# Rounding weights in the background of a matmul stage: loads asked further ahead, four raw tiles and two high tiles in rotation

## The chip, the cores and the metric

One core of a Trainium2 chip. The metric is the device time of one execution in microseconds, as the median of three runs. The core has five engines with an instruction queue each: TensorE (PE: matmuls, and weight loads shown as PEld), VectorE (DVE), ScalarE (ACT), GpSimd (POOL) and SyncE (SP, which here only issues DMAs). Each engine works through its own queue in order and waits on semaphores for the others.

## The reference

One layer of a causal decoder: a half-step gated feed-forward network, two attention mixers in parallel, and a second half-step feed-forward network, on a sequence of 1024 rows of width 1024, all in float32.

```python
x = x + 0.5 * swiglu(rms_norm(x, g_ffn1), w1_gate, w1_up, w1_down)      # 1024 -> 2816 -> 1024
proj = rms_norm(x, g_mix) @ w_in                                        # one combined projection
# ... q, k, v and gates are columns of proj; attention a (sparse), attention b (stick-breaking) ...
x = x + (sigmoid(gate_a) * (y_a @ w_o_a) + sigmoid(gate_b) * (y_b @ w_o_b)) @ w_out
x = x + 0.5 * swiglu(rms_norm(x, g_ffn2), w2_gate, w2_up, w2_down)

def swiglu(h, w_gate, w_up, w_down):
    return (silu(h @ w_gate) * (h @ w_up)) @ w_down
```

## The kernel before, in words

Products are made in a reduced float32 format of the matmul engine. To keep the accuracy, every operand is split into a high part (a rounded copy) and a low part (what the rounding left), and one product of tiles is three matmuls: high by high, high by low and low by high (lines L468 to L470).

The kernel runs in stages. The one that matters here is the first gate and up stage, `ffn_in("a", ...)`: silu(h @ w1_gate) * (h @ w1_up). The 2816 columns are taken 256 at a time, as eleven pairs p of two 128-column blocks. The first pair is done plainly (`opening`). For each of the ten others the gate (e = 0) and the up half (e = 1) are each one fast matrix product of 2 x 2 blocks that takes 7 block products instead of 8 (`products`). A block product is `times`: 4 blocks of depth times 3 matmuls, 12 matmuls of 128x128 by 128x512. So the stage has 10 x 2 x 7 = 140 block products behind the opening, in sequences of seven. In a sequence the products have the places 0 to 6 (the order 1, 6, 7, 5, 2, 4, 3 of the fast scheme) and go to the PSUM banks pa, pb, pc, pd, pa, pc, pd. Between the places 0 and 4 ScalarE copies bank pa out (L481); between 3 and 6 VectorE adds bank pd to a sum (L491) before the product at place 6 goes on accumulating in it. VectorE also makes the sums of the next sequence's left sides (L457 to L460), ScalarE rounds these and the weights themselves (L377), GpSimd subtracts to get the low parts (L378). SyncE loads weights (L440, tiles a0r and a1r, 512 KB each) and stores finished results to DRAM (L594, `staged`).

Beside this work the stage does a background job (`beside`, called after each block product): it prepares 24 column blocks of w_in that later stages need, in high and low parts, in DRAM. They come in two pieces each, 48 pieces of 128x512. A piece goes through four steps:

- load: SyncE loads 256 KB into a raw tile `swr` (L799);
- split: ScalarE copies it rounded into a high tile `swh` (L789), and VectorE subtracts it from the raw tile in place, so that this then holds the low part (L790);
- store: SyncE stores the high part (L793, targets named ..hd) and the low part (..ld), one after the other.

`behind` ties a step to a block product: the load, the split's rounding and the store each wait for that product's last matmul. Before the change three slots take turns. A tuple in `points` gives the places of split, store and load of a slot:

```python
spare = in_turn((c3, 3), (c1, 1), (pair, 2))
held, points = {}, ((0, 1, 3), (2, 3, 5), (4, 5, 0))
```

So every sequence of seven products does three pieces: splits after the places 0, 2 and 4, each store one product behind its split, and the load of the slot's next piece two products behind that store, 4 products ahead of its own split. A slot has a raw tile and a high tile of its own, six tiles in all, handed out by `spare`. A load can't start before the store of the low part has left the raw tile.

Semaphores and the order of the instructions on each engine are made by a planner, from the traced order, the data dependences, the added ones of `behind`, and its own estimate of times. Only the opening is held to its written order as a whole, and a few instructions by `keep_in_program_order`.

Of the kernel before, what the change touches and what calls it, by code (L numbers as in the profile page):

```python
# [23 lines left out]
P = 128  # L24
# [33 lines left out]
def f32(ap):  # L58
    return ap.bitcast(F32)
# [186 lines left out]
def trunk(ctx, tc, x, positions, g_ffn1, w1_gate, w1_up, w1_down, g_mix, w_in, g_cq, w_uq_a, w_q_idx,  # L246
          g_q_a, g_k_a, w_uv_a, w_o_a, w_o_b, w_out, g_ffn2, w2_gate, w2_up, w2_down, inv_freq, out):
    nc = tc.nc
# [28 lines left out]
    def column(g, n, name):  # L277
        t = cst.tile([P, n], F32, name=name)
        nc.sync.dma_start(t, g[0].rearrange("(k p) -> p k", p=P))
        return t  # L280
# [31 lines left out]
    def in_turn(*sources):  # L312

        order = [f for n in range(max(n for f, n in sources)) for f, m in sources if n < m]
        at = [0]

        def tile_(name):
            at[0] += 1
            return order[(at[0] - 1) % len(order)](name)

        return tile_
# [59 lines left out]
    class Right:  # L381
# [16 lines left out]
        def place(self, xs, half, junk=None):  # L398

            self.x, self.half, self.junk, self.rs = xs, half, junk, {}  # L400
            for q in range(2):
                self.y[half, q] = ([xt[:, q * 512:q * 512 + 512] for xt in xs] if half else
                                   [self.ct(f"{self.nm}y{q}{t}") for t in range(4)])
# [33 lines left out]
    def loader(raw, nm):  # L437
        def load(w, f, name):
            t = raw(name)
            nc.sync.dma_start(t.rearrange("p (k f) -> p k f", k=ND),  # L440
                              w[0, :, f * P:(f + 1) * P].rearrange("(k p) f -> p k f", p=P))
            return t

        return load

    def ffn_in(nm, R, wg, wu, raw, op, sums, ct, bank, staged, rows, first=None, beside=lambda n, ins: None):
# [26 lines left out]
        def mul(O, n, ps, start=True):  # L473
            a, b = FACTORS[n]
            beside("1675243".index(str(n)), times(O[a], B[b], ps, start))
# [253 lines left out]
    columns = {f"wg{g}": C_GA + g * P for g in (*range(ND, 2 * ND), *range(ND))}  # L729
    columns.update((f"wqk{base}{pr}", base + pr * P) for pr in range(4) for base in (C_QB, C_KB))  # L730
    split_of = {nm: [dram.tile([P, 1024], F32, name=f"{nm}{part}d") for part in "hl"] for nm in columns}
    rows_of = w_in[0].rearrange("(k p) f -> p k f", p=P)
# [18 lines left out]
    def ring(pool):  # L751

        op = in_turn((wt, 4), (lambda name: pool.tile([P, 1024], F32R, tag="r", name=name, bufs=NR), NR))
        raw = in_turn((rawt, 2), (lambda name: pool.tile([P, 1024], F32, tag="raw", name=name, bufs=2), 2))
        return op, raw

    def of(pool, tag, bufs, n=1024, dt=F32):
        return lambda name: pool.tile([P, n], dt, tag=tag, name=name, bufs=bufs)
# [3 lines left out]
    with tc.tile_pool(name="ring1", bufs=1) as rpool, tc.tile_pool(name="s1", bufs=1) as spool, tc.tile_pool(name="ps1", bufs=1, space=PSUM) as psum:  # L762
        op, raw = ring(rpool)
        bank = banks(psum)
        sums, pair = of(spool, "s", 5, 512), of(spool, "pair", 2, 512, F32R)
        with tc.tile_pool(name="t1", bufs=1, side="right") as tpool, tc.tile_pool(name="c1", bufs=1) as cpool:
            tt = of(tpool, "t", 28, dt=F32R)
            fp = lambda place: lambda name: f32(place(name))

            c4, c5, c3, c1 = (of(cpool, f"c{n}", n, 512, F32R) for n in (4, 5, 3, 1))  # L770
            ct = fp(in_turn(*[(f, 1) for f in [c4] * 4 + [c5] * 5]))
            spare = in_turn((c3, 3), (c1, 1), (pair, 2))
            R = Right(g_ffn1, bank, fp(op), fp(in_turn((c5, 5), (c3, 3))), tt, "a")
            xs = []

            pieces = [(nm, c) for nm in columns for c in range(0, 1024, 512)]
            held, points = {}, ((0, 1, 3), (2, 3, 5), (4, 5, 0))

            def behind(ins, *others):
                for o in others:  # L780
                    tc.add_manual_dep(o.ins, ins.ins.name, mybir.DependencyInfo(
                        mybir.DependencyClass.Sync, mybir.DependencyReason.DATA), reason="pace")

            def beside(n, ins):

                for slot, (split_, store, load_) in enumerate(points):
                    if n == split_ and slot in held:
                        nm, c, raw, hi = held[slot]
                        behind(ins, nc.scalar.activation(hi, raw, AF.Copy))  # L789
                        nc.vector.tensor_tensor(raw, raw, f32(hi), op=ALU.subtract)  # L790
                    if n == store and slot in held:
                        nm, c, raw, hi = held.pop(slot)
                        behind(ins, *(nc.sync.dma_start(d[:, c:c + 512], part)  # L793
                                      for d, part in zip(split_of[nm], (f32(hi), raw))))
                    if n == load_ and pieces:
                        nm, c = pieces.pop(0)
                        raw, hi = f32(spare(f"swr{slot}")), spare(f"swh{slot}")
                        held[slot] = nm, c, raw, hi
                        behind(ins, nc.sync.dma_start(raw.rearrange("p (k f) -> p k f", f=P),  # L799
                                                      rows_of[:, c // P:(c + 512) // P, columns[nm]:columns[nm] + P]))  # L800

            def rows(t):
                xs.append(fp(tt)(f"x{t}"))
                nc.sync.dma_start(xs[t], x[0, t * P:(t + 1) * P, :])

            load = loader(raw, "a")
            for t in range(4):
                rows(t)
                if t == 1:
                    R.gain()  # L810
            first = [[load(w, q, f"a{e}r0") for q in range(2)] for e, w in enumerate((w1_gate, w1_up))]
            for t in range(4, NT):
                rows(t)
            gcolm = column(g_mix, ND, "gcolm")
            gcolq = column(g_cq, QR // P, "gcolq")
            gk = cst.tile([P, HD], F32, name="gk")
            nc.sync.dma_start(gk, g_k_a[0].partition_broadcast(P))

            R.place(xs[0:4], 0)
            R.stat(0)  # L820
            for t in range(4):
                if t < 3:
                    R.stat(t + 1)
                R.norm(t)
            R.second = lambda: R.place(xs[4:8], 1, sums)
            ffn_in("a", R, w1_gate, w1_up, raw, op, sums, ct, bank, staged[0], range(4), first, beside)
            assert not held and not pieces
        hpool.append(tc.tile_pool(name="hpool", bufs=1, side="right"))
        hstack = ExitStack()
        hpool[0] = hstack.enter_context(hpool[0])  # L830
# [129 lines left out]
    fp = tc.tile_pool(name="sf", bufs=1)  # L960
# [1055 lines left out]
    with tc.tile_pool(name="ring2", bufs=1) as rpool, tc.tile_pool(name="ps6", bufs=1, space=PSUM) as psum:  # L2016
        op, raw = ring(rpool)
        bank = banks(psum)
        with tc.tile_pool(name="m0", bufs=1) as mpool:
            M0 = []  # L2020
            for d in range(0, ND, 2):
                wh, wl = first.pop(0) if first else wcols(w_o_a, d * P, 2 * P, 0, 4, f"woa{d}")
                for e in range(2):
# [5 lines left out]
                    for k in range(4):  # L2029
                        c = slice((2 * k + e) * P, (2 * k + e + 1) * P)  # L2030
# [9 lines left out]
            fp = lambda place: lambda name: f32(place(name))  # L2040
# [132 lines left out]
```

## Time and profile before

| | us |
|---|---|
| median of 3 runs | 2239.9 |
| range of the runs | 2239.87 to 2240.59 |
| profiled execution, its own time | 2240.86 |
| its span, first to last instruction | 2239.1 |
| mean granted TensorE clock | 0.989 of full |
| TensorE busy, of the span | 97% |
| VectorE, ScalarE, GpSimd busy | 68%, 49%, 38% |

Rows of the profile name a line (L789 is line 789 of the kernel), an engine, an operation, and output tile <- input tiles with their buffer numbers left out. An engine name with q (SPq) is its instruction queue. In a row of a group stand the count, the busy time in us with the mean duration of one in ns, and the time for which the engine sat idle just before these instructions, with what ended most of that time. In a row of the timeline stand start and duration in us, and in brackets the idle time before the instruction and what ended it. In a row of waits stand the total, the number of times and the longest, in us. The releasers are inferred: of several semaphores the row names the one that came last by the profile.

### The profile page before, as it was taken

The numbers are of one execution on the slowest core, as the hardware profiler recorded it, in microseconds if no ns is written. First come the engines' busy times: TensorE is split into PE (matmuls) and PEld (weight loads), VectorE is DVE, ScalarE is ACT, GpSimd is POOL, SyncE is SP. The second block draws the span as 40 slices with busy tenths as digits, with TensorE's granted clock in tenths as the row PEclk, the third lists the DMA queues.
The fourth block names the chain that finished last, engine by engine and source line by source line (L and its number), as shares of the span: only waits on it lengthen the run. The fifth ranks groups of instructions, "written<-read, shape, count | busy, mean of one in ns | idle before, by whom it ended". The sixth has DMA issues, their size and how long they took to land.

```text
span 2239.1 us, 30578 instructions
## 1 busy us (share of the span) xinstructions
PE 2169.2 (97%) x10460; PEld 1807.1 (81%) x10460; DVE 1526.3 (68%) x2548; ACT 1104.4 (49%) x2169; POOL 858.2 (38%) x698
## 2 busy tenths in 40 slices
PE   7999999999999999899999899999999999999999
PEld 6887787788878988788788788877888888888877
DVE  5675675687875498677788688853465564668685
ACT  4333333334445258999989466533333232233443
POOL 3355455532236344211111322255245454552233
PEclk9999999999999999999999999999999999999999
DMA  5376676688686333665554623566223233349755
GB/s 171 99 216 199 205 239 190 195 286 275 198 219 177 111 118 126 195 176 170 151 160 164 209 95 99 170 218 236 67 77 117 90 113 97 115 160 324 229 165 184
DMA packets 269052, 381.01 MB, mean 170 GB/s; under 512 B 23264, under 2 KB 157040, under 8 KB 268896
## 3 DMA queue, kind: packets, MB, share of 16 engines
q1 hardware_dynamic: 256384, 339.17, 48.9%
q0 software_dynamic: 12512, 39.89, 4.9%
q8 instruction: 82, 1.34, 0.2%
q14 instruction: 74, 0.61, 0.1%
HBM read 259.94 MB, written 119.05 MB: 169 GB/s over the span
## 4 chain that ended last, share of the span: by engine, by line
PE 70%; ACT 7%; DVE 6%; DMA 4%; issue 3%; POOL 2%; SPq 0%; ACTq 0%; POOLq 0%; DVEq 0%
PE p L681 6%; PE p L682 6%; PE p L680 6%; ACT junka L1186 3%; PE pd L468 3%; PE pd L469 3%; PE pd L470 3%; PE pc L470 3%; PE pc L468 3%; PE pc L469 3%; PE pa L469 3%; PE pa L468 3%; PE pa L470 3%; PE psf L308 2%; PE psf L309 2%
## 5 line engine op out<-in xcount | busy, mean ns | idle before, releaser
L1186 ACT ACTIVATE junka<-u,cand,sig 128x768 bf16<-128x768 f32 (+4 forms) x186 | 183.8, 988 | 5.6 <-DVE cand L1183 4.0
L790 DVE TENSOR_TENSOR swr<-swr,swh 128x512 f32<-128x512 f32 x48 | 45.8, 954 | 111.2 <-ACT swh L789 107.2
L789 ACT ACTIVATE swh<-swr 128x512 fp32r<-128x512 f32 x48 | 30.2, 630 | 165.6 <-DMA swr<-in_w_in_dram 56.5
L1627 DVE TENSOR_TENSOR_SCAN left<-left 128x640 f32<-128x640 f32 (+3 forms) x64 | 86.3, 1349 | 4.0 <-ACT left L1619 4.0
L1120 POOL DMA_DIRECT2D gd<-evg x32 | 17.9, 560 | 152.6 <-ACT evg L1117 112.7
L1676 DVE TENSOR_TENSOR pt<-pstT,pt 128x512 fp32r<-128x512 f32 (+1 forms) x96 | 50.8, 549 | 28.6 <-ACT pt L1674 28.3
L584 ACT ACTIVATE b0u<-b0u 128x512 f32<-128x512 f32 x20 | 12.7, 633 | 95.3 <-DVE b0u L491 78.9
L1676 DVE TENSOR_TENSOR pt<-pspT,pt 128x512 fp32r<-128x512 f32 x72 | 46.8, 684 | 16.3 <-ACT pt L1674 16.3
L681 PE MATMUL p<-bT,bS 128*128 128x512 f32 x132 | 52.5, 398 | 2.4 <-DVE bT L378 2.4
L1674 ACT ACTIVATE pt<-pspT 128x512 fp32r<-128x512 f32 x72 | 39.7, 596 | 29.2 <-PE pspT L1886 29.1
L1807 ACT ACTIVATE e<-e,nm 128x256 f32<-128x256 f32 (+7 forms) x64 | 49.3, 773 | 9.3 <-DVE nm L1802 9.2
L1540 DVE SCALAR_TENSOR_TENSOR u<-relu,WI,u 128x512 f32<-128x512 f32 (+1 forms) x70 | 50.1, 733 | 5.2 <-ACT relu L1533 4.6
L1795 DVE CUSTOM_DVE_ANT_0 e<-psL,bias 128x512 f32<-128x512 f32 (+3 forms) x96 | 49.7, 550 | 5.5 <-PE psL L1832 5.5
L682 PE MATMUL p<-bT,bS 128*128 128x512 f32 x132 | 51.9, 396 | 1.0 <-POOL bS L378 1.0
L681 PE MATMUL p<-aT,aS 128*128 128x512 f32 x132 | 51.5, 390 | 0.0
L1630 DVE TENSOR_TENSOR sa<-sa,left 128x639 f32<-128x639 f32 (+3 forms) x64 | 48.1, 752 | 3.7 <-ACT sa L1621 0.2
L682 PE MATMUL p<-aT,aS 128*128 128x512 f32 x132 | 50.4, 389 | 0.0
L1674 ACT ACTIVATE pt<-pstT 128x512 fp32r<-128x512 f32 (+1 forms) x96 | 47.1, 519 | 3.3 <-PE pstT L1730 3.1
L1533 ACT ACTIVATE relu<-psdot 128x512 f32<-128x512 f32 (+1 forms) x80 | 40.1, 520 | 17.4 <-DVE u L1540 8.6
L1886 PE MATMUL pspT<-ident,e 128*128 128x128 f32 x288 | 39.6, 277 | 8.1 <-DVE ri L1809 5.5
L1619 ACT ACTIVATE left<-psz 128x512 f32<-128x512 f32 (+2 forms) x96 | 46.2, 505 | 2.0 <-PE psz L1654 1.8
L1621 ACT ACTIVATE sa<-psz 128x512 f32<-128x512 f32 (+2 forms) x96 | 47.0, 511 | 0.1
(3021 smaller groups left out, 8247.8 us busy)
## 6 DMA issues: line engine op xcount, KB each, us to landing
aw<-in_w_down_dram SPq DMA_DIRECT2D x33, 512.0 KB, 4.9
bw<-in_w_down_dram SPq DMA_DIRECT2D x33, 512.0 KB, 5.0
swr<-in_w_in_dram SPq DMA_DIRECT2D x48, 256.0 KB, 5.1
a0r<-in_w_gate_dram SPq DMA_DIRECT2D x22, 512.0 KB, 6.7
a1r<-in_w_up_dram SPq DMA_DIRECT2D x22, 512.0 KB, 7.2
b0r<-in_w_gate_dram SPq DMA_DIRECT2D x22, 512.0 KB, 4.2
b1r<-in_w_up_dram SPq DMA_DIRECT2D x22, 512.0 KB, 3.9
x<-in_x_dram SPq DMA_DIRECT2D x16, 512.0 KB, 6.1
```

The source lines that it names most:

```text
L468: nc.tensor.matmul(ps, a[:, c], b[k][:, HI], start=start and k == 0, stop=False, skip_group_check=True)
L469: nc.tensor.matmul(ps, a[:, c], b[k][:, LO], start=False, stop=False, skip_group_check=True)
L470: ins = nc.tensor.matmul(ps, a[:, l], b[k][:, HI], start=False, stop=k == 3, skip_group_check=True)
L680: nc.tensor.matmul(ps[q][m], S[:, h], T[:, HI], start=p == 0, stop=False)
L681: nc.tensor.matmul(ps[q][m], S[:, h], T[:, LO], start=False, stop=False)
L682: nc.tensor.matmul(ps[q][m], S[:, l], T[:, HI], start=False, stop=p == last)
L1186: nc.scalar.activation(junks[1][:, 0:(i + 1) * P], score[i], AF.Sign, scale=sig[:, b:b + 1], bias=cand.bitcast(F32)[:, b:b + 1], accum_out ...
L1540: nc.vector.scalar_tensor_tensor(ac, r, wv, ac, op0=ALU.mult, op1=ALU.add)
L1627: nc.vector.tensor_tensor_scan(back, back, back, 1.0, op0=ALU.mult, op1=ALU.bypass)
L1674: nc.scalar.activation(pt[:, off:512], tp[:, off:512], AF.Copy)
L1676: nc.vector.tensor_sub(pt[:, 512 + off:1024], tp[:, off:512], f32(pt[:, off:512]))
L1795: nc.vector.tensor_tensor_reduce(e[:, c], lp[:, 0:n_], bias[:, c], 1.0, LOW, op0=ALU.add, op1=ALU.max, accum_out=m)
```

## The change

The slots go. Pieces are numbered k, and `splits` gives the block product, counted through the stage from 0, after which piece k is split: 7, 9, 11, 14, 16, 18, and so on, the places 0, 2 and 4 of each sequence from the second on. `agenda` maps a product to the steps behind it. The store stays one product behind the split. The load of piece k comes 3 products behind the split of piece k - 4, that is 2 behind its store as before; the first four are asked after the products 0 to 3. From a load to its own split there are thus 6 or 7 products. The six tiles are divided otherwise: four raw tiles in rotation (`early`, from c3 and c1), taken when the load is asked, and two high tiles in rotation (`late`, from `pair`), taken when the split is made. The traced order within one product follows the order in which the steps were appended to `agenda`: a store or split of an earlier piece ahead of a load of a later one.

```diff
-            spare = in_turn((c3, 3), (c1, 1), (pair, 2))
+            early, late = fp(in_turn((c3, 3), (c1, 1))), pair
...
-            held, points = {}, ((0, 1, 3), (2, 3, 5), (4, 5, 0))
+            splits = [7 * (k // 3 + 1) + (0, 2, 4)[k % 3] for k in range(len(pieces))]
+            agenda, held, halved, turn = defaultdict(list), [], [], [0]
+            for k, n in enumerate(splits):
+                agenda[n].append("split")
+                agenda[n + 1].append("store")
+                agenda[splits[k - 4] + 3 if k > 3 else k].append("load")
...
             def beside(n, ins):
 
-                for slot, (split_, store, load_) in enumerate(points):
-                    if n == split_ and slot in held:
-                        nm, c, raw, hi = held[slot]
+                at, turn[0] = turn[0], turn[0] + 1
+                for step in agenda.pop(at, ()):
+                    if step == "load":
+                        nm, c = pieces.pop(0)
+                        raw = early("swr")
+                        held.append((nm, c, raw))
+                        behind(ins, nc.sync.dma_start(raw.rearrange("p (k f) -> p k f", f=P),
+                                                      rows_of[:, c // P:(c + 512) // P, columns[nm]:columns[nm] + P]))
+                    elif step == "split":
+                        nm, c, raw = held.pop(0)
+                        hi = late("swh")
                         behind(ins, nc.scalar.activation(hi, raw, AF.Copy))
                         nc.vector.tensor_tensor(raw, raw, f32(hi), op=ALU.subtract)
-                    if n == store and slot in held:
-                        nm, c, raw, hi = held.pop(slot)
+                        halved.append((nm, c, raw, hi))
+                    else:
+                        nm, c, raw, hi = halved.pop(0)
                         behind(ins, *(nc.sync.dma_start(d[:, c:c + 512], part)
                                       for d, part in zip(split_of[nm], (f32(hi), raw))))
-                    if n == load_ and pieces:
-                        nm, c = pieces.pop(0)
-                        raw, hi = f32(spare(f"swr{slot}")), spare(f"swh{slot}")
-                        held[slot] = nm, c, raw, hi
-                        behind(ins, nc.sync.dma_start(raw.rearrange("p (k f) -> p k f", f=P),
-                                                      rows_of[:, c // P:(c + 512) // P, columns[nm]:columns[nm] + P]))
```

More of the change, by code (lines that the diff above doesn't have):

```diff
@@ L826, in trunk @@
             ffn_in("a", R, w1_gate, w1_up, raw, op, sums, ct, bank, staged[0], range(4), first, beside)
-            assert not held and not pieces
+            assert not agenda and not held and not halved and not pieces
         hpool.append(tc.tile_pool(name="hpool", bufs=1, side="right"))
```

## The prediction

> **What bounds the kernel now.** I read the page first.
>
> ```profile
> span 2239.1 us, 30578 instructions
> ...
> PE 2169.2 (97%) x10460; PEld 1807.1 (81%) x10460; DVE 1526.3 (68%) x2548; ACT 1104.4 (49%) x2169; POOL 858.2 (38%) x698
> ...
> L790 DVE TENSOR_TENSOR swr<-swr,swh 128x512 f32<-128x512 f32 x48 | 45.8, 954 | 111.2 <-ACT swh L789 107.2
> L789 ACT ACTIVATE swh<-swr 128x512 fp32r<-128x512 f32 x48 | 30.2, 630 | 165.6 <-DMA swr<-in_w_in_dram 56.5
> ...
> swr<-in_w_in_dram SPq DMA_DIRECT2D x48, 256.0 KB, 5.1
> ```
>
> TensorE is busy 97% of the span, so only a wait that reaches TensorE is worth time. The background rounding is where ScalarE and VectorE wait most: 165.6 us before L789, 111.2 us before L790. Idle time there is free until TensorE wants something queued behind it, so next come TensorE's own waits from 75 to 430 us, then the busy time of two stretches (columns: start to end, length, TensorE busy and its instructions, weight loads, VectorE, ScalarE, GpSimd, clock, DMA share, GB/s), and two matmuls 82 issues apart followed by the next stage's first.
>
> ```profile
> PE pd L468 <- DVE a1u L491: 9.9, 4, 4.4
> PE pa L468 <- ACT a1u L481: 3.3, 1, 3.3
> PE pc L470 <- POOL a09S L378: 0.4, 1, 0.4
> PE pb L470 <- POOL a04S L378: 0.2, 1, 0.2
> ```
>
> ```profile
> 80.80:186.00 105.20, 105.20 (x465) 87.09 (x464) 63.09 (x81) 36.94 (x67) 53.93 (x37) 1.00 0.70 201
> ```
>
> ```profile
> 75.27:478.43 403.16, 389.32 (x1684) 319.00 (x1683) 262.37 (x325) 140.16 (x254) 211.18 (x140) 0.98 0.69 205
> ```
>
> ```profile
> 459.61 0.39 PE L469 MATMUL pa<-aB,a110A 128*128 128x512 f32 x1
> ...
> 478.20 0.39 PE L470 MATMUL pd<-aB,a110S 128*128 128x512 f32 x1
> 478.43 0.39 PE L680 MATMUL p<-aT,aS 128*128 128x512 f32 x1
> ```
>
> The stage's 140 products are 1680 matmuls, in the 403.16 us from 75.27 to 478.43 (the other 4 are transposes). The full pace is (478.20 - 459.61) / 82 = 0.2267 us, so a product takes 12 x 0.2267 = 2.72 us and all of them 380.9 us. About 22 us is lost: 403.16 - 389.32 = 13.84 us is idle, nearly all in five stalls; the rest is slow matmuls. The first 105 us have no idle time at all, and the next stage follows without a gap: what TensorE saves here is passed on.
>
> Now the late splits on ScalarE, each with the idle time before it, and the VectorE instructions behind one of them:
>
> ```profile
> 186.84 0.63 ACT L789 ACTIVATE swh<-swr 128x512 fp32r<-128x512 f32 x1 [6.92 <-DMA wg14ld<-swr]
> ...
> 224.52 0.63 ACT L789 ACTIVATE swh<-swr 128x512 fp32r<-128x512 f32 x1 [7.21 <-DMA swr<-in_w_in_dram]
> ...
> 234.01 0.63 ACT L789 ACTIVATE swh<-swr 128x512 fp32r<-128x512 f32 x1 [8.37 <-DMA a1r<-in_w_up_dram]
> ```
>
> ```profile
> 354.74 0.63 ACT L789 ACTIVATE swh<-swr 128x512 fp32r<-128x512 f32 x1 [10.06 <-DMA wqk5201ld<-swr]
> ...
> 396.65 0.63 ACT L789 ACTIVATE swh<-swr 128x512 fp32r<-128x512 f32 x1 [6.48 <-DMA a1r<-in_w_up_dram]
> ```
>
> ```profile
> 234.67 0.69 DVE L790 TENSOR_TENSOR swr<-swr,swh 128x512 f32<-128x512 f32 x1 [7.40 <-ACT swh L789]
> 235.28 0.68 DVE L491 TENSOR_TENSOR a1u<-a1u,pd 128x512 f32<-128x512 f32 x1
> ```
>
> ```profile
> 225.69 0.50 PE L468 MATMUL pa<-aB,a14A 128*128 128x512 f32 x1 [3.31 <-ACT a1u L481]
> ...
> 229.67 0.39 PE L469 MATMUL pa<-aB,a14A 128*128 128x512 f32 x1
> ...
> 236.01 0.51 PE L468 MATMUL pd<-aB,a14S 128*128 128x512 f32 x1 [3.01 <-DVE a1u L491]
> ...
> 240.46 0.40 PE L468 MATMUL pa<-aB,a05A 128*128 128x512 f32 x1
> ```
>
> ```profile
> 356.74 0.79 PE L468 MATMUL pd<-aB,a17S 128*128 128x512 f32 x1 [4.38 <-DVE a1u L491]
> ...
> 362.79 0.40 PE L470 MATMUL pa<-aB,a08A 128*128 128x512 f32 x1
> ```
>
> The chain can be read off. At 234.01 the split starts, at 234.67 L790, at 235.28 L491 (which empties bank pd), and at 236.01 TensorE, 2.00 us behind the split; at 354.74 and 356.74 it is 2.00 us again. For bank pa the split at 224.52 holds back L481, and TensorE resumes at 225.69, 1.17 us later. A split after product n leaves three products, 8.16 us, before TensorE returns to the bank, so it may be 8.16 - 2.00 = 6.2 us late (7.0 for pa) at no cost. Every us beyond stops TensorE.
>
> Why it is late stands in the SyncE queue:
>
> ```profile
> 207.61 0.71 SPq L793 DMA_DIRECT2D wg0ld<-swr  x1
> 216.28 0.38 SPq L799 DMA_DIRECT2D swr<-in_w_in_dram  x1
> 216.77 0.44 SPq L793 DMA_DIRECT2D wg0hd<-swh  x1
> 217.63 0.32 SPq L793 DMA_DIRECT2D wg0ld<-swr  x1
> 225.82 0.38 SPq L799 DMA_DIRECT2D swr<-in_w_in_dram  x1
> 226.30 0.46 SPq L793 DMA_DIRECT2D wg1hd<-swh  x1
> ```
>
> ```profile
> SPq L799 <- DMA wg0ld<-swr: 15.7, 2, 7.9
> ```
>
> ```profile
> L789 ACT ACTIVATE swh<-swr x48: 614/632/635, 92.7 to 410.9; 128x512 fp32r<-128x512 f32 x48
> ```
>
> ```profile
> DMA to landing us min/median/max: 3.7/5.3/11.1
> ```
>
> (The last row covers tile swh, so the stores of the high parts.) Each load stands right behind the store of the low part whose tile it refills, and waits there until that store has landed, up to 7.9 us; the next piece's stores wait behind it. One piece therefore costs the queue about 0.38 + 0.46 + 0.38 + 5.3 = 6.5 us, with three pieces in 7 products (6.35 us each). Measured: (410.9 - 92.7) / 47 = 6.77 us. The background sets the pace and TensorE is held to it: (6.77 - 6.35) x 47 = 19.7 us, nearly what the stage loses.
>
> **The change, part by part.** Loads, splits, subtractions, stores and bytes are the same in number, and the same six tiles serve: as instructions it costs nothing.
>
> *Lead.* A load is asked 6 or 7 products before its split instead of 4: 5.44 us earlier or more. By itself that exceeds the largest stall (4.38) and leaves something only where two follow each other: those at 225.69 and 236.01 add to 3.31 + 1.7 + 3.01 = 8.0 us.
>
> *Order on SyncE.* Store and load of one raw tile remain two products apart, but the entries between them change. After product 3 of a sequence, store(1) is now traced ahead of the load that waits for store(0); after product 5, store(2) ahead of the load that waits for store(1). The store awaited is two products old (5.44 us) against a landing of 5.3 us, and its successor is already out. Only the load after product 0 has the newest store in front of it, 5.44 us old as well. If the queue were the limit, two pieces would now fit in the 6.5 us of one. So I take the wait at L799 as near nothing; its upper end is today's 7.9 us, which the longer lead then has to cover.
>
> *Two high tiles instead of three.* This is the added wait: a split waits until the high part of two pieces ago has been stored. That store is asked 4 products (10.9 us) before the split, or 3 (8.2 us) for the split after product 4. Landing 5.3 us in the median: nothing. The longest, 11.1 us: 2.9 us late, inside the 6.2. Behind the waiting split stand L481, L582 and the halving at L377, and so TensorE. With a SyncE wait of 7.9 us on top: 7.9 + 11.1 - 8.2 - 6.2 = 4.6 us of stall. I take nothing, being nearest to the median row.
>
> *Weights.* Earlier loads pass the weight loads on SyncE.
>
> ```profile
> L377 ACT ACTIVATE a15A<-a1r x3: 613/618/619, 241.5 to 259.2; 128x512 fp32r<-128x512 f32 x3
> ...
> L440 SPq DMA_DIRECT2D a1r<-in_w_up_dram x2: 431/639/847, 227.3 to 227.8; - x2
> ```
>
> A weight pair asked at 227.3 is first read at 241.5: one more 256 KB transfer (5.1 us) ahead of it is hidden in those 14.2 us. Were that cover gone, those 5.1 us would stall TensorE once.
>
> *Ends.* The first split comes after product 7 instead of 4, the last after 116 instead of 114, of 140: nothing waits for it there.
>
> *Slow matmuls.* From 225.69 to 229.67 ten issues take 3.98 us instead of 2.27; from 236.01 to 240.46 twelve take 4.45 instead of 2.72; from 356.74 to 362.79 fourteen take 6.05 instead of 3.17. Excess 1.71 + 1.73 + 2.88 = 6.3 us; it goes with the stalls.
>
> The Trainium skill ("TensorE: Matmul & The Clock Gate", section "HAM oscillation — how this bites in real kernels") lets the clock fall to half only for idle gaps of more than about 3.4 us. By it only the 4.38 us stall would be followed by slow matmuls, and the sum would be 3.4 us smaller, at about 2223; the rows show them after 3.01 and 3.31 us too, so I keep 6.3.
>
> *Sum.* The profiled execution took 2240.86 us: 2240.86 - 13.84 - 6.3 = 2220.7. The median of the runs, 2239.9, is 0.96 lower, which gives 2219.8. I allow 0.7 us for a split that is still late: **2220.5 us**.
>
> **Rivals.**
>
> *The queue stays the limit.* If the planner, which orders SyncE by its own estimate, puts each load ahead of the next store again, the 6.5 us per piece remain. At the measured 6.77 us only the 5.44 us of lead are gained (2234.5); at 6.5 us the lag is (6.5 - 6.35) x 47 = 7.1, less 5.44, so 1.7 us lost (2221.5). I take the middle, 2228. For it: that order stands in the rows now. Against it: it is the traced order now, and the trace changes.
>
> *The high tiles turn too short: slower.* It decides at the split after product 4, once a high store lands over 8.2 + 6.2 = 14.4 us after it is asked. A stall then costs 4.6 us plus some 2.1 of slow matmuls (6.3 / 3), 6.7 in all. Three cancel the gain; six give 2219.8 + 6 x 6.7 = 2260. For it: landing of 11.1 us exists, and stores stand behind waiting loads. Against it: it takes the longest landing and the longest wait together, repeatedly.
>
> *Nothing moves.* Were the loads in time already, with something else releasing the splits, the time would stay at 2240. For it: rows name other tiles (a1r) as the release. Against it: those releases are inferred, and the SyncE rows show the loads stuck.
>
> The Trainium skill ("DMA: Bandwidth & Descriptors", section "Anatomy of one DMA — SWDGE (gpsimd) path") has 2.0 us plus the bytes at 436 GB/s, an estimate of 2.6 us for 256 KB. By it a lead of 4 products is ample and this rival holds, at 2240; the trace has 5.1 us, so it gets little.
>
> **How the numbers follow.** Forecast (2216 to 2225, one small stall left or none): 0.70. Queue stays the limit: 0.14. Nothing moves: 0.08. High tiles: 0.08. A measurement here can tell about 0.2% (4.5 us) from no change. The first two are faster but for the last end of the second; so faster 0.84, same 0.08, slower 0.08. The range reaches from the whole 22 us and a little of shifted order later (2215) to near the upper end of the second case (2233), 0.82 or so.
>
> **What would show it.** Right: no wait of TensorE on L491 or L481 over 1 us between 75 and 430 us, no matmuls at 0.43 us there, the first L680 some 20 us earlier (near 458), idle time before L789 far below 165.6 us with little of it on swr loads, and on SyncE a store pair ahead of each waiting load. The queue rival shows as splits still 6.6 us or more apart on average; the high-tile rival as L789 waiting on swh stores (hd) by more than 6 us with stalls behind. The forecast is wrong if the first L680 is early but the end isn't, or if new stalls name weights (L377 on a0r or a1r).

## The result, and the profile after

| | before | after |
|---|---|---|
| median of 5 runs | 2239.9 | 2218.59 |
| range | 2237.29 to 2240.59 | 2216.34 to 2219.96 |
| profiled execution, own time | 2240.86 | 2216.60 |
| first matmul of the next stage (L680) | 478.4 | 457.2 |

The ratio is 0.9904 (95% interval 0.989 to 0.9917): 21.3 us faster, against 19.4 forecast. The page of the changed kernel, whose split is now L802 and whose subtraction is L803 (the load is L797, the stores L807):

```profile
span 2214.8 us, 30577 instructions
...
PE 2156.8 (97%) x10460; PEld 1800.9 (81%) x10460; DVE 1524.3 (69%) x2548; ACT 1103.8 (50%) x2169; POOL 858.1 (39%) x698
...
L802 ACT ACTIVATE swh<-swr 128x512 fp32r<-128x512 f32 x48 | 30.2, 628 | 117.2 <-issue 47.8
...
L803 DVE TENSOR_TENSOR swr<-swr,swh 128x512 f32<-128x512 f32 x48 | 41.1, 856 | 43.0 <-ACT swh L802 42.9
```

ScalarE still sits idle 117.2 us before its splits, but mostly for nothing that the profile shows ("issue", 47.8 us) or for TensorE (47.7 us, in its view of waits): most splits now have their data and wait for the product that they are tied to. Late loads account for 8.5 us of it, high tiles not yet stored for 13.0. The stage, by busy time of the engines, and its end:

```profile
75.27:457.20 381.93, 381.93 (x1693) 316.41 (x1691) 261.69 (x325) 141.25 (x256) 211.91 (x141) 1.00 0.74 216
```

```profile
456.93 0.39 PE L470 MATMUL pd<-aB,a110S 128*128 128x512 f32 x1
457.16 0.39 PE L680 MATMUL p<-aT,aS 128*128 128x512 f32 x1
```

TensorE is busy through all of it, at full clock, and its view of waits from 75 to 430 us has no row left. The stage ends 21.2 us earlier, nearly the whole of the 22 us that it lost. The profiled execution is another 3 us faster behind it; that execution was one of the two fastest of five, and in the profiles below the rest of the span, from the first L680 to the end, is 1757.6 to 1762.4 us whatever the kernel, so I take the 3 us for scatter.

The SyncE queue, where the loads and stores stand:

```profile
208.68 0.38 SPq L797 DMA_DIRECT2D swr<-in_w_in_dram  x1
209.17 0.45 SPq L807 DMA_DIRECT2D wg0hd<-swh  x1
209.73 0.36 SPq L807 DMA_DIRECT2D wg0ld<-swr  x1
210.19 0.41 SPq L797 DMA_DIRECT2D swr<-in_w_in_dram  x1
211.01 4.60 SPq L440 DMA_DIRECT2D a1r<-in_w_up_dram  x2
218.34 0.45 SPq L797 DMA_DIRECT2D swr<-in_w_in_dram  x1
218.88 0.80 SPq L807 DMA_DIRECT2D wg1hd<-swh  x1
219.77 0.38 SPq L807 DMA_DIRECT2D wg1ld<-swr  x1
220.75 0.32 SPq L807 DMA_DIRECT2D wg1hd<-swh  x1
221.12 0.63 SPq L807 DMA_DIRECT2D wg1ld<-swr  x1
```

Before, a load came 8 to 9 us behind the store ahead of it (207.61 to 216.28, 217.63 to 225.82). Now a load is issued 0.1 us behind a store (209.73 to 210.19), because the store it waits for is an older one. All of SyncE's waits of loads for low stores, summed over the rows of its view of waits from 75 to 480 us, were 134.5 us before and are 42.2 us now, in 17 waits of at most 4.7 us.

### The profile page after: what moved, and what is told of

Read it like the earlier page. It is cut to its first block, busy times and chain, and to the rows that moved or that the text cites. A ratio compares the mean times of both kernels' runs of the same rounds, so it can differ in the third digit from the quotient of the medians.

```text
span 2214.8 us, 30577 instructions
## 1 busy us (share of the span) xinstructions
PE 2156.8 (97%) x10460; PEld 1800.9 (81%) x10460; DVE 1524.3 (69%) x2548; ACT 1103.8 (50%) x2169; POOL 858.1 (39%) x698
## 4 chain that ended last, share of the span: by engine, by line
PE 80%; ACT 7%; DVE 6%; DMA 3%; issue 2%; POOL 1%; SPq 0%; ACTq 0%; DVEq 0%; POOLq 0%
PE p L681 6%; PE p L682 6%; PE p L680 5%; PE pc L468 4%; PE pd L468 4%; PE pd L469 4%; PE pd L470 4%; PE pc L469 4%; PE pc L470 4%; PE pa L468 3%; PE pa L469 3%; PE pa L470 3%; ACT junka L1194 3%; PE psf L308 2%; PE psf L309 2%
## 5 line engine op out<-in xcount | busy, mean ns | idle before, releaser
L802 ACT ACTIVATE swh<-swr 128x512 fp32r<-128x512 f32 x48 | 30.2, 628 | 117.2 <-issue 47.8
L803 DVE TENSOR_TENSOR swr<-swr,swh 128x512 f32<-128x512 f32 x48 | 41.1, 856 | 43.0 <-ACT swh L802 42.9
```

## Experiments

The change does three things at once: loads are asked 6 or 7 products ahead of the split instead of 4 (theory L: this lead brings the gain), they are traced behind the next piece's store instead of ahead of it (theory Q: the order in the SyncE queue brings it), and four raw and two high tiles serve instead of three and three. Ratios are to the kernel before on the same chip; a time at the scale of the table above is ratio x 2239.9.

| run | lead | load and next store in SyncE | raw, high tiles | ratio (95%) | load waits for low stores, us | first L680 |
|---|---|---|---|---|---|---|
| before | 4 | load first | 3, 3 | 1 | 134.5 | 478.4 |
| after | 6 to 7 | store first | 4, 2 | 0.9904 | 42.2 | 457.2 |
| e1_order | 4 | store first | 3, 3 | 0.9894 (0.9877 to 0.9911) | 40.0 | 456.4 |
| e2_loads_first | 6 to 7 | load first | 4, 2 | 1.0013 (1.0004 to 1.0023) | 166.2 | 480.3 |
| e3_lead4 | 4 | store first | 4, 2 | 0.9910 (0.9896 to 0.9925) | 0 | 456.7 |
| e9_later | 3 | store first | 3, 3 | 0.9903 (0.9889 to 0.9918) | 16.6 | 457.8 |

**Order alone.** The kernel before, with stores traced ahead of loads behind each product.

```diff
                 for slot, (split_, store, load_) in enumerate(points):
                     if n == split_ and slot in held:
...
+                for slot, (split_, store, load_) in enumerate(points):
                     if n == store and slot in held:
...
+                for slot, (split_, store, load_) in enumerate(points):
                     if n == load_ and pieces:
...
```

> The kernel before with one thing changed: behind each block product the stores are traced ahead of the loads. Lead stays 4 products, three raw and three high tiles. Theory Q (a load that stands right behind the store it waits for holds up the SyncE queue, 6.5 us per piece): the two loads behind places 3 and 5 now have a younger store ahead of them, the pieces need less than 6.35 us each, splits are late by less than 6.2 us, and most of the gain is here, 2218 to 2224 us, TensorE idle on L491 and L481 under 2 us. Theory L (only the longer lead takes the lateness away): little changes, 2233 to 2240 us, stalls of 10 us or more remain.

Measured: 2216.9 us, ratio 0.9894, 1 us below theory Q's range. The whole gain is here, with lead and tiles as they were. The split is L789 in this kernel, the load L801, the store L794. Its row of ScalarE's groups from 75 to 480 us, and its SyncE queue:

```profile
L789 ACT ACTIVATE swh<-swr 128x512 fp32r<-128x512 f32 x48 | 30.1, 628 | 119.4 <-DMA swr<-in_w_in_dram 44.7 <-PE pc L470 29.7 <-PE pa L470 21.4
```

```profile
207.97 0.32 SPq L794 DMA_DIRECT2D wg1hd<-swh  x1
208.40 0.37 SPq L794 DMA_DIRECT2D wg1ld<-swr  x1
208.86 0.40 SPq L801 DMA_DIRECT2D swr<-in_w_in_dram  x1
```

Splits still wait 44.7 us for loads, more than after the change (8.5 us in its view of waits), yet TensorE has no wait at all: the lateness stays inside the slack.

**The longer lead in the old order.** The changed kernel with the load traced ahead of the store behind a product. It keeps the four raw and two high tiles, so it is not the lead alone.

```diff
-                for step in agenda.pop(at, ()):
+                for step in sorted(agenda.pop(at, ()), key=lambda s: s != "load"):
```

> The changed kernel with one thing undone: behind each block product the load is traced ahead of the store, as in the kernel before; lead 6 to 7 products, four raw and two high tiles stay. Theory Q: the queue is again held 6.5 to 6.8 us per piece, more than the 6.35 that TensorE leaves, so stalls come back late in the stage when the longer lead is used up: 2221 to 2234 us, middle 2228, waits of the loads for the low stores (..ld) 100 us or more in all. Theory L: the lead alone covers it, 2217 to 2220 us, no stall.

Measured: 2242.22 us, ratio 1.0013. Nothing of the gain is left; the result is worse than theory Q's range. TensorE's waits from 75 to 480 us begin with these rows, and the SyncE queue shows the old picture:

```profile
PE pd L468 <- DVE a1u L491: 9.7, 3, 4.5
PE pc L468 <- ACT a14S L377: 1.9, 1, 1.9
PE pa L468 <- ACT a1u L481: 1.4, 1, 1.4
```

```profile
207.43 0.71 SPq L807 DMA_DIRECT2D wg15ld<-swr  x1
215.61 0.38 SPq L797 DMA_DIRECT2D swr<-in_w_in_dram  x1
216.09 0.46 SPq L807 DMA_DIRECT2D wg0hd<-swh  x1
216.64 0.38 SPq L807 DMA_DIRECT2D wg0ld<-swr  x1
224.00 0.38 SPq L797 DMA_DIRECT2D swr<-in_w_in_dram  x1
```

The first split starts at 93.9 and the last at 424.0: (424.0 - 93.9) / 47 = 7.02 us per piece, slower than before (6.77), where TensorE leaves 6.35. Both contain TensorE's own stalls. What the splits wait for has changed: loads are the releaser of 8.1 us, stores of high parts of 126.5 us (summed over the rows of ScalarE's waits). The two high tiles don't come free, because their stores stand behind the waiting loads. The lead does put the stalls off: TensorE's first wait of over 1 us ends at 188.9 before and at 216.8 here.

**The high stores out of that queue.** As the last, with the high part stored from ScalarE's queue behind its rounding; SyncE stores the low part only.

```diff
                         behind(ins, nc.scalar.activation(hi, raw, AF.Copy))
+                        nc.scalar.dma_start(split_of[nm][0][:, c:c + 512], f32(hi))
...
-                        behind(ins, *(nc.sync.dma_start(d[:, c:c + 512], part)
-                                      for d, part in zip(split_of[nm], (f32(hi), raw))))
+                        behind(ins, nc.sync.dma_start(split_of[nm][1][:, c:c + 512], raw))
```

> The kernel of the run with loads traced first (lead 6 to 7, load right behind the store it waits for), but the high part is stored from the ScalarE queue right behind its rounding, so it no longer stands behind a waiting load on SyncE. Theory H (in that run the splits were late because the stores of the high parts were held up in the SyncE queue and the two high tiles weren't free): stalls go although SyncE goes on waiting 100 us or more for low stores, 2217 to 2224 us. Theory R (the raw loads themselves come too late in that order): stalls of 8 us or more remain, 2232 us or more.

Measured: 2233.66 us, ratio 0.9967 (0.9954 to 0.998), with 10.0 us of waits of TensorE. By time this is what theory R had (2232 us or more), but part of the loss went. 1.0013 - 0.9967 = 0.0046, some 10 us, went with the high stores (the edit also takes their issue, 0.46 us each, off SyncE); the rest stays. ScalarE's waits name it:

```profile
ACT swh L802 <- DMA swr<-in_w_in_dram: 57.5, 12, 9.9
```

The raw loads themselves come late although asked 6 or 7 products ahead. SyncE waits 183.1 us for low stores, and a piece takes (415.4 - 95.1) / 47 = 6.81 us. So neither H nor R was the whole of it. A queue that is slower than the work it feeds uses up the lead, and the longer lead decides when: TensorE's first wait of over 1 us ends at 251.2 here.

**Lead 4 in the changed kernel.**

```diff
-                agenda[splits[k - 4] + 3 if k > 3 else k].append("load")
+                agenda[n - 4].append("load")
```

> The changed kernel with every load asked 4 products ahead of its split, as before the change, with four raw and two high tiles; the load then stands 5 or 6 products behind the store that frees its tile, so it never waits for it. Theory Q: 10.9 us cover the landing of 5 to 6 us, no stall, 2217 to 2221 us. Theory L: the short lead brings the late splits back, 2230 to 2240 us.

Measured: 2219.47 us, ratio 0.9910, no wait of TensorE in the stage. As theory Q has it. (By the edit a load stands 4 or 5 products behind the store that frees its tile; the 5 or 6 above count from the split.)

**Asked later, and faster.** The kernel before, each load one product later.

```diff
-            held, points = {}, ((0, 1, 3), (2, 3, 5), (4, 5, 0))
+            held, points = {}, ((0, 1, 4), (2, 3, 6), (4, 5, 1))
```

> The kernel before with one number per slot changed: each load is asked one product later, 3 products behind the store of its tile and only 3 ahead of its own split (8.2 us). The next piece's store now stands between a store and the load that waits for it. Theory Q (holding up the SyncE queue is the whole loss): although the loads are asked later, the time falls to 2217 to 2228 us; SyncE's waits for low stores fall from 134 us to under 50. Theory L (how far ahead a load is asked decides): slower than before, 2243 us or more.

Measured: 2219.07 us, ratio 0.9903; the loads wait 16.6 us for low stores. In the queue the load at 206.29 waits for the store at 199.89, and a younger pair of stores (202.24, 202.87) is already out ahead of it:

```profile
199.89 0.49 SPq L793 DMA_DIRECT2D wg0ld<-swr  x1
200.53 0.38 SPq L799 DMA_DIRECT2D swr<-in_w_in_dram  x1
202.24 0.32 SPq L793 DMA_DIRECT2D wg0hd<-swh  x1
202.87 0.32 SPq L793 DMA_DIRECT2D wg0ld<-swr  x1
206.29 0.38 SPq L799 DMA_DIRECT2D swr<-in_w_in_dram  x1
```

A load that is asked 2.7 us later makes the kernel 22 us faster, as much as the change does. That a longer lead is needed (theory L) is refuted; Q holds. This edit both puts a store between and gives the awaited store more time; order alone does only the first.

**How little lead is enough.** Leads of 3, 2 and 1 products in the changed kernel (the line of the lead 4 run with 3, 2 and 1).

> The changed kernel with every load asked 3 products (8.2 us) ahead of its split; between the run with 4 products (2219 us, no stall) and that with 2 (2237 us). Loads land 6 us after they are asked in the median, 13 us at worst: the worst is 5 us late, inside the slack of 6.2 us unless SyncE holds the load back as well. Expected 2218 to 2226 us, at most two stalls.

> The changed kernel with every load asked 2 products (5.4 us) ahead of its split. Landing 5 to 6 us in the median, so the usual split is up to 1 us late and the slowest loads (13 us) 8 us late. By the slack of 6.2 us worked out for a late split, at most one or two stalls of a few us: 2218 to 2226 us, ScalarE waiting 60 us or more for loads. If the slack is smaller than that, stalls in most sequences, 2235 us or more.

> The changed kernel with every load asked 1 product (2.7 us) ahead of its split: the usual split is 3 us late (inside 6.2 us), those of loads that land after 9 us stall TensorE. By the slack: 2220 to 2236 us with some stalls of 1 to 5 us; if the slack doesn't hold, 2240 us or more.

Measured: 2220.28 us with 3 (ratio 0.9904, 0.9887 to 0.992; no wait of TensorE), 2237.0 us with 2 (0.9978, 0.9966 to 0.999), 2300.15 us with 1 (1.0263, 1.0247 to 1.0278). The curve has its edge between 3 and 2 products. For 2 and 1 I expected too little loss: both times are those that I had put to a smaller slack. With lead 2, ScalarE and TensorE:

```profile
227.36 0.63 ACT L802 ACTIVATE swh<-swr 128x512 fp32r<-128x512 f32 x1 [7.85 <-DMA swr<-in_w_in_dram]
234.93 0.63 ACT L802 ACTIVATE swh<-swr 128x512 fp32r<-128x512 f32 x1 [6.46 <-DMA swr<-in_w_in_dram]
```

```profile
228.53 0.50 PE L468 MATMUL pa<-aB,a14A 128*128 128x512 f32 x1 [1.84 <-ACT a1u L481]
...
236.94 0.50 PE L468 MATMUL pd<-aB,a14S 128*128 128x512 f32 x1 [1.04 <-DVE a1u L491]
```

The slack is not smaller: the way from the late split to TensorE is as predicted, 1.17 us to bank pa and 2.01 us to bank pd. The lateness was mis-sized. The loads behind these splits, and what stood ahead of them:

```profile
215.72 0.32 SPq L807 DMA_DIRECT2D wg0hd<-swh  x1
217.48 0.32 SPq L807 DMA_DIRECT2D wg0ld<-swr  x1
217.84 0.43 SPq L797 DMA_DIRECT2D swr<-in_w_in_dram  x1
218.69 2.81 SPq L440 DMA_DIRECT2D a1r<-in_w_up_dram  x2
221.56 5.77 SPq L797 DMA_DIRECT2D swr<-in_w_in_dram  x1
```

A load issued at 217.84, ahead of 1 MB of weights, released its split at 227.36, 9.5 us later against the 6.2 us median landing of that run; the next one's issue alone took SyncE 5.77 us behind the weights. And the load of 217.84 was itself held up: the product that it is tied to was through at about 213, but it stood behind the stores of the piece before, whose split started only at 215.06. SyncE waits 67.3 us in this run for splits to end, so with a short lead the queue is held again, this time by the stores. I had counted landing, not these.

**One high tile.** The changed kernel with one high tile, and with three raw tiles and one place that alternates between two.

```diff
-            early, late = fp(in_turn((c3, 3), (c1, 1))), pair
+            early, late = fp(in_turn((c3, 3), (pair, 1))), c1
```

> The changed kernel with one high tile instead of two (the freed tiles go to the raw rotation, three plus one place that alternates between two). A split now waits for the high store of the piece just before, asked one product (2.7 us) earlier where splits are two products apart, so with landing of about 5 us most splits are 2 to 4 us late. If a split may be 6.2 us late at no cost, as worked out, TensorE loses under 4 us: 2217 to 2223 us, though ScalarE waits 80 us or more for ..hd stores. If the high tiles are a live danger as the slower rival has it, stalls appear: 2235 us or more.

Measured: 2254.99 us, ratio 1.0068 (1.0053 to 1.0083). This is the slower rival, made real. SyncE, ScalarE and TensorE around one of its nine stalls:

```profile
208.10 0.74 SPq L797 DMA_DIRECT2D swr<-in_w_in_dram  x1
208.94 1.97 SPq L594 DMA_DIRECT2D staged<-a1u  x1
210.99 0.38 SPq L594 DMA_DIRECT2D staged<-a1c  x1
211.43 0.45 SPq L594 DMA_DIRECT2D staged<-a0u  x1
211.98 0.50 SPq L807 DMA_DIRECT2D wg15hd<-swh  x1
```

```profile
207.02 0.63 ACT L802 ACTIVATE swh<-swr 128x512 fp32r<-128x512 f32 x1 [6.10 <-DMA wg15hd<-swh]
...
219.18 0.63 ACT L802 ACTIVATE swh<-swr 128x512 fp32r<-128x512 f32 x1 [11.04 <-DMA wg15hd<-swh]
```

```profile
221.18 0.79 PE L468 MATMUL pd<-aB,a04S 128*128 128x512 f32 x1 [5.42 <-DVE a0u L491]
```

The high part is ready at 207.65, but its store is issued at 211.98, behind stores of results that VectorE finishes between 208.2 and 210.0 (L594), the first of which takes 1.97 us to issue. It lands some 7 us later, the split starts at 219.18, and TensorE 2.00 us after it. Whether the queue or the landing costs this, the next run tells: the same, with the high part stored from ScalarE's queue (the edit shown above).

> The kernel of the run with one high tile, with the high part stored from the ScalarE queue right behind its rounding. If the loss there (some 36 us against the changed kernel) came from the high stores standing in the SyncE queue behind results that wait for VectorE, it goes: the store is asked at the split, 5.4 us or more before the next split, landing 3 to 5 us, 2217 to 2224 us. If one tile is too few by the landing time alone, 2235 us or more.

Measured: 2217.78 us, ratio 0.9899 (0.9884 to 0.9914), no wait of TensorE in the stage. One high tile is enough when its store doesn't stand in SyncE's queue.

## Why the prediction was right, point by point

- **What bounds the kernel**: right. The five stalls and the slow matmuls behind them are gone, and nothing else took their place; the stage now runs at the pace of its matmuls. The 19.7 us were weaker evidence than I took them for: a split waits for its product, so the 6.77 us between splits contain TensorE's own stalls. That the queue set the pace is shown by the run with the order alone.
- **Slack of a late split, 6.2 and 7.0 us**: the constants behind it (2.00 and 1.17 us) returned in every profile with such stalls, and 44.7 us of waiting for loads (order alone) or 59.2 (lead 3) cost TensorE nothing.
- **Lead**: the step that failed. I gave the 5.44 us a worth of their own, "by itself that exceeds the largest stall". With the old order the kernel with the longer lead still has stalls of up to 4.5 us and is not faster than before (1.0013), and with the new order 3, 4 and 6 products give the same time. With the high stores out of the queue the longer lead stands beside a gain of 0.33% (0.9967) in the old order, which TensorE still pays for with a wait of 6.0 us; how much of that gain is the lead's is not shown. No run has the longer lead with the old order and three high tiles. The sum came out because it holds no term for the lead alone, and the other cause covers it.
- **Order on SyncE**: right, and the whole effect. That two pieces would fit where one did can't be read from these runs, since TensorE sets the pace again; that loads hold the queue far less can: 134.5 us of waits became 42.2. That is not the "near nothing" I took, but the rest never reached TensorE.
- **Two high tiles**: nothing, as taken, in the new order (13.0 us of ScalarE's waits on them, none reaching TensorE). In the old order they cost up to 10 us, by the run with the high stores out of the queue, which I hadn't seen: I priced the SyncE wait once, not as the regular state.
- **Weights and ends**: TensorE had no wait on them. But I read the weights only for what a load does to them. Before the change five loads right behind a pair of weight loads took 3.4 to 7.0 us to issue. Three of them (issued at 182.64, 228.75 and 347.61, for 3.87, 5.05 and 7.03 us) were through 2.1 to 2.3 us before three of the five stalls ended (188.85, 236.01, 356.74). So the weights may set where the held queue reaches TensorE; no run takes this apart.
- **Slow matmuls, 6.3 us**: went with the stalls; the 21.2 us that the stage gained contain them. The 2223 us that followed from the rule of the Trainium skill quoted in the prediction were further off.
- **Size**: 20.1 us taken from the stage, less 0.7 for a split still late, against 21.2 measured. The 0.7 was an allowance that no row gave; no split was late enough to need it, and 1.1 us that I had not attributed to a stall went too.
- **Rivals**: "the queue stays the limit" did not occur, as the traced order held, but the lead 6 run with loads first shows its price: 1.0013 x 2239.9 = 2243 instead of the 2228 I put on it, since the held queue also starves the high tiles. With these fed from elsewhere it is 0.9967 x 2239.9 = 2232.5, near the 2234.5 of that rival's upper end. "High tiles too short" lives one tile further down. "Nothing moves" held a true half: the lead was not what was short. What was late was the issue, and that moved. The 2.6 us that the prediction sets beside this rival rest on a figure that the Trainium skill ("DMA: Bandwidth & Descriptors", section "Anatomy of one DMA — SWDGE (gpsimd) path") gives for DMAs of GpSimd's path. SyncE issues these loads, and they land in 5.1 us in the median before the change and in 6.0 after it.

## What to carry to other kernels

In a queue that works in order, look at what stands right behind a waiting entry before you look at how early the entry was asked: a load whose buffer is freed by the store just ahead of it turns the landing time of every store into queue time. Put the next piece's stores between a store and the load that reuses its buffer. And divide: the queue's time per piece (here 6.5 us by its entries) against the pace of the work beside it (6.35 us). If it is longer, more lead only delays the stalls. How early a load is asked counts once it is too short: here 2 products instead of 3 cost 17 us.

## What the runs showed of the hardware that I had not expected

A stall of TensorE is followed by a stretch of slow matmuls or by none, and among the short stalls the length alone doesn't decide. Two stalls, of the run with lead 2 and of that with one high tile:

```profile
228.53 0.50 PE L468 MATMUL pa<-aB,a14A 128*128 128x512 f32 x1 [1.84 <-ACT a1u L481]
...
229.95 0.63 PE L469 MATMUL pa<-aB,a14A 128*128 128x512 f32 x1
...
232.51 0.41 PE L469 MATMUL pa<-aB,a14A 128*128 128x512 f32 x1
```

```profile
113.38 0.50 PE L468 MATMUL pd<-aB,a11S 128*128 128x512 f32 x1 [2.27 <-DVE a1u L491]
...
115.78 0.39 PE L469 MATMUL pd<-aB,a11S 128*128 128x512 f32 x1
```

After 1.84 us of idle time ten matmuls took 3.98 us instead of 2.27; after 2.27 us of idle time ten took 2.40. The granted clock over these ten was 0.57 and 1.00. Over the profiles of six kernels every stall of 3.0 us or more was followed by a slow stretch that cost 1.7 to 3.0 us, stalls of 1.84, 1.90, 2.12 and 2.22 us too, and stalls of 2.27, 2.49 and 2.83 us not, nor any of 1.80 us or less. (The Trainium skill, "TensorE: Matmul & The Clock Gate", section "HAM oscillation — how this bites in real kernels", has gaps of more than about 3.4 us; here shorter ones did it as well.) So about 2 us of idle time can cost twice its length. Why one does and another doesn't was not settled.
